# Splitting the first weights behind each layer normalisation one step earlier, into spare activation tiles

## The chip, the core and the metric

The kernel runs on one core of a Trainium2 chip. TensorE (PE) multiplies, VectorE (DVE) and ScalarE (ACT) work on tiles, GpSimd (POOL) can do some of the same work, and SyncE (SP) issues the weight transfers from HBM. Each engine works through its own queue in order. The metric is the device time of one execution in microseconds (us); lower is better.

## What is computed

Two decoder layers on 256 tokens of width 2048, all in float32. Cut to what matters here:

```python
def layer_norm(x, g, b):
    mu = jnp.mean(x, axis=-1, keepdims=True)
    var = jnp.mean(jnp.square(x - mu), axis=-1, keepdims=True)
    return (x - mu) * lax.rsqrt(var + LN_EPS) * g + b

for l in range(2):
    h = gated_deltanet(x, ...) if l == 0 else diff_attention(x, ..., k_sh, v_sh)   # ends in @ w_out or @ w_o
    x = layer_norm(ALPHA * x + h, ln_g[l, 0], ln_b[l, 0])
    x = layer_norm(ALPHA * x + square(relu(x @ w_up[l])) @ w_down[l], ln_g[l, 1], ln_b[l, 1])
    if l == 0:
        k_sh, v_sh = split(x @ w_kv)
return x
```

Four normalisations stand in this order. Behind each of the first three comes a matrix product that needs the whole normalised row: `w_up` of layer 0, `w_kv`, and `w_up` of layer 1. They are called LN1, LN2 and LN3 below. Behind the fourth comes only the output.

## The kernel before, in words

**Tiling.** The 256 tokens are two tiles of 128 (`t` = 0, 1). A product (`gemm`, one entry of `self.plan`) takes 16 weight blocks of 128x1024 (`k` = 0 to 15, one 512 KB transfer each) and makes 1024 output columns, as two groups of 512 (`g` = 0, 1) in PSUM tiles `acc`. Float32 is split in two: `wh` is the weight rounded to float32r by an ACT cast (line 78) and `wl` the rest, by a DVE subtraction (line 79); the activations are split likewise in `xhl` (the normalised stream, features on partitions) or in `blk` tiles (other activations). One block, one `t` and one `g` then take three PE instructions (lines 174 to 176): xh*wh, xh*wl, xl*wh.

**Steps.** `run` walks over steps of 4 to 6 blocks (`cuts`). A step makes the products of its blocks for `t` = 0, then asks `load_weights` for the blocks of the next step, then makes the products for `t` = 1. So while one step multiplies, the next one is transferred and split. `wr` tiles, into which SP transfers, are four; `wh` and `wl` tiles are six each. A transfer can only be issued when the `wr` tile of four blocks before has been split, and a cast only when the `wh` tile of six blocks before has been multiplied. The pool `blk` has 11 tiles of 128x2048.

**The normalisation.** The product ahead of each normalisation ends in `residual`. In its last step of 6 blocks, the products of `t` = 0 come first, those of `t` = 1 after them, one group `g` after the other. As each `acc` is complete, DVE adds it to the residual row `self.r[t]` (line 293) and takes statistics (line 295). When a row tile is complete, `ln_stats` forms the scale in eight small DVE instructions (lines 255 to 256 and 100 to 103), and `ln_apply(ln, t, q)` normalises quarter `q` (512 columns, four blocks `k`): two DVE instructions (lines 265 and 266), then four PE transposes (line 204), an ACT cast and a DVE subtraction into `xhl`. Quarters 0 and 1 of a row tile are applied directly; quarters 2 and 3 of both are applied behind quarters 0 and 1 of `t` = 1.

**Order around it.** `self.after(ins)` puts what is recorded in its block behind `ins` on that engine. `self.hold` is the last instruction of `ln_stats`; the weights split next are put behind it. While `hold` is set, `load_weights` (called with `share`) gives every odd `k` to POOL instead of DVE. The first product behind a normalisation has steps of 6, 5 and 5 blocks. Tile framework and queues keep the recorded order only roughly: a scheduler sets each engine's final order.

Of the kernel before, what the change touches and what calls it, by code (L numbers as in the profile page):

```python
# [11 lines left out]
F32R = mybir.dt.float32r  # L12
# [6 lines left out]
P = 128  # L19
T = 256  # L20
NT = T // P
D = 2048
KD = D // P
DFF = 8192
C = 1024
G = 512
NG = C // G
SC = 4
# [7 lines left out]
class Trunk:  # L36
# [77 lines left out]
    def act_stat(act):  # L114
        return lambda k, part, t: Trunk.act_view(act[k // 4])[:, part, t, k % 4]

    def gemm(self, nk, wsrc, stat, evac, pre=None, rate=1, need=None, cuts=None):

        self.plan.append((nk, wsrc, stat, evac, pre, rate, need, cuts or [SC] * (nk // SC)))

    def run(self):
        steps = [(i, sum(gm[7][:n]), c) for i, gm in enumerate(self.plan) for n, c in enumerate(gm[7])]
        loaded, self.hold = {}, None
        self.load_weights(loaded, *steps[0])
        acc = {}
        for j, (i, s, n) in enumerate(steps):
            nk, _, stat, evac, pre, rate, need, _ = self.plan[i]
            if s == 0:
                acc = {}
                if pre is not None:  # L130
                    pre()
            if need is not None:
                need(s)
            ws = loaded.pop((i, s))
            for t in range(NT):

                turns = [(g,) for g in range(NG)] if s + n >= nk and t == NT - 1 else [range(NG)]
                for gs in turns:
                    for n_, (k, wh, wl) in enumerate(ws):
                        self.product(acc, k, nk, t, gs, wh, wl, stat)  # L140
                        if n_ and self.pending:
                            fn, args = self.pending.popleft()
                            with self.after(self.last):
                                fn(*args)
                    if s + n >= nk:
                        for g in gs:
                            evac(g, t, acc[g, t])
                if t == 0 and j + 1 < len(steps):
                    with self.after(self.hold):
                        self.load_weights(loaded, *steps[j + 1], self.hold is not None)  # L150
                    self.hold = None
                self.pump(rate)

    def load_weights(self, loaded, i, s, n, share=False):
        wsrc = self.plan[i][1]
        ws = []
        for k in range(s, s + n):
            wr = self.raw.tile([P, C], F32, name="wr")
            self.nc.sync.dma_start(wr, wsrc(k))
            wh = self.hi.tile([P, C], F32R, name="wh")  # L160
            wl = self.lo.tile([P, C], F32R, name="wl")
            self.split(wh, wl, wr, self.nc.gpsimd if share and k % 2 else None)
            ws.append((k, wh, wl))
        loaded[i, s] = ws

    def product(self, acc, k, nk, t, gs, wh, wl, stat):
# [120 lines left out]
    def residual(self, n, alpha, ln=None):  # L287


        def ev(gi, t, ps):  # L290
            q = n * NG + gi
            rc = self.r[t][:, q * G : (q + 1) * G]
            self.nc.vector.scalar_tensor_tensor(rc, rc, alpha, ps, op0=ALU.mult, op1=ALU.add)  # L293
            if ln is not None:
                self.nc.vector.bn_stats(ln["st"][t][:, q], rc)
                if q == D // G - 1:
                    self.ln_stats(ln, t)
                    with self.after(ln["end"]):
                        if ln["out"] is not None:
                            self.ln_finish(ln, t, 2 + t)  # L300
                        elif t == 0:
                            self.ln_apply(ln, 0, 0)
                            self.ln_apply(ln, 0, 1)
                        else:
                            self.ln_apply(ln, 1, 0)
                            self.ln_apply(ln, 1, 1)
                            for n_ in range(2, D // G):
                                self.ln_apply(ln, 0, n_)
                                self.ln_apply(ln, 1, n_)
                    self.hold = ln["end"]  # L310

        return ev
# [21 lines left out]
    def mlp(self, w_up, w_down, g, b, out=None):  # L334
        NQ = 4
        FQ = DFF // NQ
        ln = dict(g_src=g, b_src=b, out=out)
        for f in range(NQ):
            h = []

            def up(n, h=h):
                def ev(gi, t, ps):
                    if t == 0:
                        h.append(self.blk(F32R))
                    a = self.sm()
                    self.nc.scalar.activation(a, ps, AF.Relu)  # L346
                    self.nc.vector.tensor_tensor(a, a, a, op=ALU.mult)  # L347
                    self.soon(self.to_features, a, self.act_view(h[n * NG + gi]), t)

                return ev  # L350

            last = f == NQ - 1
            for n in range(FQ // C):
                self.gemm(
                    KD, self.cols(w_up, f * FQ + n * C), self.x_stat, up(n), cuts=[6, 5, 5] if f == n == 0 else None
                )
            for n in range(D // C):
                self.gemm(
                    FQ // P, self.cols(w_down, n * C, f * FQ), self.act_stat(h),
                    self.residual(n, ALPHA if f == 0 else 1.0, ln if last else None),  # L360
                    pre=(lambda: self.ln_load(ln)) if last and n == 0 else None,
                    cuts=self.ends(n) if last else None,
                )
# [395 lines left out]
    def diff_attention(self, w_kv, w_q, lam_params, subln_w, w_o, g, b, out=None):  # L759
# [27 lines left out]
        def heads(name, follow=None):  # L787


            def ev(gi, t, ps):  # L790
                if (gi, t) == (0, 0):
                    st[name] = self.blk().rearrange("p (h t) -> p h t", h=8)
                a = self.sm()
                nc.scalar.copy(a, ps)
                self.soon(turned, gi, t, a)

            def turned(gi, t, a):
                nc.vector.tensor_copy(st[name][:, gi * 4 : gi * 4 + 4, t * P : (t + 1) * P], self.transpose4(a))
                if follow is not None and (gi, t) == (NG - 1, NT - 1):
                    follow()  # L800

            return ev
# [71 lines left out]
        def q_heads(hh):  # L874
            def follow():
                for h in range(0, 8, 2):
                    for tt in range(NT):
                        self.later(score, st["k"], st["q"], hh, h, tt)

            return heads("q", follow)  # L880
# [13 lines left out]
        for hh in range(2):  # L894
            self.gemm(
                KD, self.cols(w_kv, hh * C), self.x_stat, heads("k"), pre=constants if hh == 0 else None,
                cuts=[6, 5, 5] if hh == 0 else None,
            )
            self.gemm(KD, self.cols(w_q, hh * C), self.x_stat, q_heads(hh))
        for hh in range(2):  # L900
# [53 lines left out]
```

## Time and profile before

| | |
|---|---|
| median of 3 runs | 2472.16 us (2465.31 to 2475.14) |
| the profiled execution, its own time | 2465.03 us |
| its span, first to last instruction | 2463.3 us |
| mean granted TensorE clock | 0.992 |
| DVE busy | 1497.2 us (61%) |
| ACT busy | 1078.2 us (44%) |
| POOL busy | 90.3 us (4%) |

The profiled execution lies at the lower end of the runs. A group of instructions in the page stands with its line, its engine, what it writes and reads (out<-in), how often it ran, its busy time and its mean. "idle before, <-releaser" is the time the engine waited and who ended the wait. PE is busy nearly all the time, but a busy PE instruction overlaps the next: a 128x512 product is shown with 0.39 us while the next starts 0.23 us after it.

### The profile page before, as it was taken

Reading aid. Unit: us, or ns where it says so; the run is one execution under the profiler, and the core shown is the slowest. Engines: PE = TensorE matmul, PEld = TensorE weight load, DVE = VectorE, ACT = ScalarE, POOL = GpSimd, SP = SyncE. Lnnn points to the kernel's source line nnn. Section 1 sums busy time; section 2 is a strip of 40 time slices with the busy share of each in tenths; the row PEclk is TensorE's granted clock in tenths of the full one; section 3 lists DMA queues with packets and bytes.
Section 4 is the critical chain, followed back from the end, with each engine's and each line's share of the span. In section 5 each row is a group of like instructions: output and inputs, shape, how many; then the busy total and the mean of one; then the engine's idle time right before and its main releaser. Section 6 shows DMA issues by size and latency. Waiting matters only on the chain.

```text
span 2463.3 us, 30465 instructions
## 1 busy us (share of the span) xinstructions
PE 2416.1 (98%) x11492; PEld 1983.3 (81%) x11492; DVE 1497.2 (61%) x2333; ACT 1078.2 (44%) x1474; POOL 90.3 (4%) x94
## 2 busy tenths in 40 slices
PE   8999999998999999999998999999999999999997
PEld 7888888887888888888887878788788888888886
DVE  4789689667554544545557575665755554555556
ACT  4545345433443433434433464643443443443442
POOL 0010010002000000000002000000200000000001
PEclk9999899999999999999999999999999999999999
DMA  6545345564555556565554545455455555656553
GB/s 229 155 139 175 98 140 160 166 233 158 188 185 191 182 194 222 172 214 182 195 197 146 180 137 171 155 174 167 161 198 195 182 190 186 217 179 214 185 195 121
DMA packets 120211, 438.84 MB, mean 178 GB/s; under 512 B 13760, under 2 KB 13792, under 8 KB 119040
## 3 DMA queue, kind: packets, MB, share of 16 engines
q1 hardware_dynamic: 115920, 420.79, 52.0%
q0 software_dynamic: 2560, 11.13, 1.4%
q10 hardware_dynamic: 1584, 4.98, 0.5%
q8 instruction: 90, 1.47, 0.2%
q14 instruction: 57, 0.47, 0.1%
HBM read 433.70 MB, written 3.15 MB: 177 GB/s over the span
## 4 chain that ended last, share of the span: by engine, by line
PE 90%; DVE 6%; DMA 2%; issue 1%; ACT 1%; POOL 0%; ACTq 0%; POOLq 0%; DVEq 0%
PE acc L174 27%; PE acc L175 27%; PE acc L176 27%; PE ps L204 3%; DVE wl L79 1%; DVE blk L266 1%; DVE blk L265 1%; PE ps L819 1%; ACT wh L78 1%; PE ps L550 1%; DMA wr<-in_gdn_w_in_dram 1%; PE ps L485 1%; DMA wr<-in_mlp_w_up_dram 0%; PE ps L621 0%; PE ps L847 0%
## 5 line engine op out<-in xcount | busy, mean ns | idle before, releaser
L79 DVE TENSOR_TENSOR wl<-wr,wh 128x1024 fp32r<-128x1024 f32 x785 | 954.5, 1227 | 675.0 <-ACT wh L78 632.1
L78 ACT CAST wh<-wr 128x1024 fp32r<-128x1024 f32 x800 | 832.1, 1052 | 945.6 <-PE acc L176 757.2
L174 PE MATMUL acc<-wh,xhl 128*128 128x512 f32 x1920 | 764.3, 398 | 0.0
L175 PE MATMUL acc<-wl,xhl 128*128 128x512 f32 x1920 | 757.7, 395 | 3.2 <-POOL wl L79 3.2
L176 PE MATMUL acc<-wh,xhl 128*128 128x512 f32 x1920 | 754.8, 393 | 0.0
L174 PE MATMUL acc<-wh,blk 128*128 128x512 f32 x1280 | 500.0, 391 | 0.0
L176 PE MATMUL acc<-wh,blk 128*128 128x512 f32 x1280 | 499.4, 390 | 0.0
L175 PE MATMUL acc<-wl,blk 128*128 128x512 f32 x1280 | 499.1, 390 | 0.0
L175 PEld LDWEIGHTS acc<-wl,xhl 128*128 128x128 f32 x1920 | 363.7, 189 | 75.7 <-POOL wl L79 4.4
L174 PEld LDWEIGHTS acc<-wh,xhl 128*128 128x128 f32 x1920 | 363.8, 189 | 73.8 <-issue 1.7
L176 PEld LDWEIGHTS acc<-wh,xhl 128*128 128x128 f32 x1920 | 362.7, 189 | 73.9
L176 PEld LDWEIGHTS acc<-wh,blk 128*128 128x128 f32 x1280 | 240.4, 188 | 50.1
L174 PEld LDWEIGHTS acc<-wh,blk 128*128 128x128 f32 x1280 | 240.4, 188 | 49.5
L175 PEld LDWEIGHTS acc<-wl,blk 128*128 128x128 f32 x1280 | 240.5, 188 | 49.2
L293 DVE SCALAR_TENSOR_TENSOR blk<-blk,acc 128x512 f32<-128x512 f32 x80 | 54.7, 685 | 85.2 <-PE acc L176 85.2
L204 PE MATMUL ps<-ident,sm 128*128 128x128 f32 x512 | 81.3, 275 | 2.5 <-DVE sm L869 1.8
L204 PEld LDWEIGHTS ps<-ident,sm 128*128 128x128 f32 x512 | 61.3, 140 | 27.3 <-PE acc L176 7.1
L78 ACT CAST blk<-ps 128x512 fp32r<-128x512 f32 x80 | 46.8, 585 | 70.9 <-PE ps L204 70.9
L347 DVE TENSOR_TENSOR sm<-sm 128x512 f32<-128x512 f32 x64 | 44.0, 691 | 52.6 <-ACT sm L346 52.2
L79 DVE TENSOR_TENSOR blk<-ps,blk 128x512 fp32r<-128x512 f32 x80 | 55.0, 688 | 30.1 <-ACT blk L78 30.1
L346 ACT ACTIVATE sm<-acc 128x512 f32<-128x512 f32 x64 | 38.2, 597 | 65.4 <-PE acc L176 62.4
L471 DVE SCALAR_TENSOR_TENSOR sm<-blk,g_cw,sm 128x255 f32<-128x255 f32 (+2 forms) x144 | 60.8, 474 | 0.0
(202 smaller groups left out, 1049.7 us busy)
## 6 DMA issues: line engine op xcount, KB each, us to landing
wr<-in_mlp_w_up_dram SPq DMA_DIRECT2D x256, 512.0 KB, 4.7
wr<-in_mlp_w_down_dram SPq DMA_DIRECT2D x256, 512.0 KB, 5.2
wr<-in_gdn_w_in_dram SPq DMA_DIRECT2D x128, 512.0 KB, 4.4
wr<-in_shared_w_kv_dram SPq DMA_DIRECT2D x64, 512.0 KB, 5.1
wr<-in_gdn_w_out_dram SPq DMA_DIRECT2D x32, 512.0 KB, 5.4
wr<-in_diff_w_q_dram SPq DMA_DIRECT2D x32, 512.0 KB, 4.6
wr<-in_diff_w_o_dram SPq DMA_DIRECT2D x32, 512.0 KB, 4.7
blk<-in_ln_g_dram POOLq DMA_DIRECT2D x4, 1024.0 KB, 7.2
```

What stands on the lines that cost most here:

```text
L78: self.nc.scalar.copy(hi, src)
L79: (engine or self.nc.vector).tensor_tensor(lo, src, hi.bitcast(F32), op=ALU.subtract)
L174: mm(ps, xh, wh[:, c], start=(k == 0), stop=False)
L175: mm(ps, xh, wl[:, c], start=False, stop=False)
L176: self.last = mm(ps, xl, wh[:, c], start=False, stop=(k == nk - 1))
L204: self.nc.tensor.transpose(pt[:, i], src[:, i * P : (i + 1) * P], self.ident)
L265: v.scalar_tensor_tensor(xc, xc, ln["mv", t][:, 0:1], ln["g"][:, c], op0=ALU.subtract, op1=ALU.mult)
L266: v.scalar_tensor_tensor(xc, xc, ln["rs", t], ln["b"][:, c], op0=ALU.mult, op1=ALU.add)
L293: self.nc.vector.scalar_tensor_tensor(rc, rc, alpha, ps, op0=ALU.mult, op1=ALU.add)
L346: self.nc.scalar.activation(a, ps, AF.Relu)
L347: self.nc.vector.tensor_tensor(a, a, a, op=ALU.mult)
L471: v_.scalar_tensor_tensor(y[:, i, d:], u[:, : T - d], w(j), y[:, i, d:], op0=ALU.mult, op1=ALU.add)
```

## The change

1. Products behind LN1, LN2 and LN3 are marked `ahead` and take steps of 5, 6 and 5 blocks.
2. Before the last step of the product ahead of the normalisation starts, `load_weights(..., big=True)` transfers and splits the five blocks of the first step behind it. They go into `blk` tiles, `wh` in one half and `wl` in the other, so no `wh`/`wl` tile is needed. At that point five `blk` tiles are free: three of the 11 not in use, and two of the four activation tiles, whose blocks have been multiplied.
3. No weight is split on POOL any more.
4. Quarters 2 and 3 of the normalisation are kept in `self.rest` as (0,2), (1,2), (0,3), (1,3) in (t, q), and are recorded inside the load of the second step: one behind its third block, one behind its sixth, the other two at the end.

```diff
-    def gemm(self, nk, wsrc, stat, evac, pre=None, rate=1, need=None, cuts=None):
+    def gemm(self, nk, wsrc, stat, evac, pre=None, rate=1, need=None, cuts=None, ahead=False):
-        self.plan.append((nk, wsrc, stat, evac, pre, rate, need, cuts or [SC] * (nk // SC)))
+        cuts = [5, 6, 5] if ahead else cuts or [SC] * (nk // SC)
+        self.plan.append((nk, wsrc, stat, evac, pre, rate, need, cuts, ahead))
...
             ws = loaded.pop((i, s))
+            if j + 1 < len(steps) and steps[j + 1][1] == 0 and self.plan[steps[j + 1][0]][8]:
+                self.load_weights(loaded, *steps[j + 1], big=True)
             for t in range(NT):
...
-                if t == 0 and j + 1 < len(steps):
+                if t == 0 and j + 1 < len(steps) and steps[j + 1][:2] not in loaded:
                     with self.after(self.hold):
-                        self.load_weights(loaded, *steps[j + 1], self.hold is not None)
+                        self.load_weights(loaded, *steps[j + 1])
...
-    def load_weights(self, loaded, i, s, n, share=False):
+    def load_weights(self, loaded, i, s, n, big=False):
...
-            wh = self.hi.tile([P, C], F32R, name="wh")
-            wl = self.lo.tile([P, C], F32R, name="wl")
-            self.split(wh, wl, wr, self.nc.gpsimd if share and k % 2 else None)
+            if big:
+                both = self.blk(F32R)
+                wh, wl = both[:, :C], both[:, C:]
+            else:
+                wh = self.hi.tile([P, C], F32R, name="wh")
+                wl = self.lo.tile([P, C], F32R, name="wl")
+            self.split(wh, wl, wr)
             ws.append((k, wh, wl))
+            if self.rest and not big and (k - s) % 3 == 2:
+                fn, args = self.rest.pop(0)
+                fn(*args)
+        while self.rest and not big:
+            fn, args = self.rest.pop(0)
+            fn(*args)
         loaded[i, s] = ws
...
-                            for n_ in range(2, D // G):
-                                self.ln_apply(ln, 0, n_)
-                                self.ln_apply(ln, 1, n_)
+                            self.rest = [(self.ln_apply, (ln, t_, n_)) for n_ in range(2, D // G) for t_ in range(NT)]
```

**What moves on the engines.** Outside the three normalisations, each engine's instructions keep their order; the three places change alike, and LN1 is shown. Lines 265, 266, 293, 295 and 204 of before are 282, 283, 310, 312 and 221 of the change; lines 174 to 176 are 191 to 193.

DVE before, where the last step ahead of LN1 is split (`wl`) and the statistics of `t` = 0 begin (`blk<-blk,acc` is the residual, `ln_st` the statistics):

```order
L79 TENSOR_TENSOR wl<-wr,wh 128x1024 x10
L293 SCALAR_TENSOR_TENSOR blk<-blk,acc 128x512 x2
L295 BN_STATS ln_st<-blk 128x6 x2
L255 BN_AGGR ln_mv<-ln_st 128x2
L256 TENSOR_SCALAR ln_rs<-ln_mv 128x1
```

DVE of the change at the same place (`blk<-wr,blk` is the `wl` half of a block split early; the third `blk<-blk,acc` belongs to `t` = 1):

```order
L79 TENSOR_TENSOR wl<-wr,wh 128x1024 x10
L79 TENSOR_TENSOR blk<-wr,blk 128x1024 x3
L310 SCALAR_TENSOR_TENSOR blk<-blk,acc 128x512
L79 TENSOR_TENSOR blk<-wr,blk 128x1024 x2
L312 BN_STATS ln_st<-blk 128x6
L310 SCALAR_TENSOR_TENSOR blk<-blk,acc 128x512
L312 BN_STATS ln_st<-blk 128x6
L310 SCALAR_TENSOR_TENSOR blk<-blk,acc 128x512
L272 BN_AGGR ln_mv<-ln_st 128x2
L312 BN_STATS ln_st<-blk 128x6
L273 TENSOR_SCALAR ln_rs<-ln_mv 128x1
```

Five subtractions now stand ahead of the statistics of `t` = 0, two of them between its first residual and its first statistics, and a residual with its statistics of `t` = 1 stand ahead of the scale of `t` = 0.

PE before, at the end of the last step ahead of LN1 (`acc<-wh,blk` multiplies activations of that product, `acc<-wh,xhl` is the first product behind the normalisation, `ps<-ident,blk` the eight transposes of quarters 0 and 1 of `t` = 0):

```order
L175 MATMUL acc<-wl,blk 128x512
L204 MATMUL ps<-ident,blk 128x128 x8
L176 MATMUL acc<-wh,blk 128x512
L174 MATMUL acc<-wh,blk 128x512
L175 MATMUL acc<-wl,blk 128x512
L176 MATMUL acc<-wh,blk 128x512
L174 MATMUL acc<-wh,blk 128x512
L175 MATMUL acc<-wl,blk 128x512
L176 MATMUL acc<-wh,blk 128x512
L174 MATMUL acc<-wh,blk 128x512
L175 MATMUL acc<-wl,blk 128x512
L176 MATMUL acc<-wh,blk 128x512
```

PE of the change there (`acc<-blk,xhl` multiplies a block split early):

```order
L193 MATMUL acc<-wh,blk 128x512
L191 MATMUL acc<-wh,blk 128x512
L192 MATMUL acc<-wl,blk 128x512
L193 MATMUL acc<-wh,blk 128x512
L221 MATMUL ps<-ident,blk 128x128 x8
L191 MATMUL acc<-blk,xhl 128x512
L192 MATMUL acc<-blk,xhl 128x512
L191 MATMUL acc<-blk,xhl 128x512
L192 MATMUL acc<-blk,xhl 128x512
L193 MATMUL acc<-blk,xhl 128x512 x2
L191 MATMUL acc<-blk,xhl 128x512
```

The transposes now stand behind the last product of the step, with nothing between them and the first product that needs them.

DVE before, from the last normalisation of quarters 2 and 3 (`blk<-blk,ln_mv` and `blk<-blk,ln_rr`, lines 265 and 266) to the second step's weights:

```order
L265 SCALAR_TENSOR_TENSOR blk<-blk,ln_mv 128x512 x2
L266 SCALAR_TENSOR_TENSOR blk<-blk,ln_rr 128x512
L79 TENSOR_TENSOR xhl<-ps,xhl 128x512
L266 SCALAR_TENSOR_TENSOR blk<-blk,ln_rr 128x512
L265 SCALAR_TENSOR_TENSOR blk<-blk,ln_mv 128x512
L79 TENSOR_TENSOR xhl<-ps,xhl 128x512
L266 SCALAR_TENSOR_TENSOR blk<-blk,ln_rr 128x512
L79 TENSOR_TENSOR xhl<-ps,xhl 128x512
L79 TENSOR_TENSOR wl<-wr,wh 128x1024
L79 TENSOR_TENSOR xhl<-ps,xhl 128x512
L79 TENSOR_TENSOR wl<-wr,wh 128x1024 x8
```

DVE of the change there, from the first block of the second step on:

```order
L79 TENSOR_TENSOR wl<-wr,wh 128x1024
L79 TENSOR_TENSOR xhl<-ps,xhl 128x512 x2
L79 TENSOR_TENSOR wl<-wr,wh 128x1024 x2
L282 SCALAR_TENSOR_TENSOR blk<-blk,ln_mv 128x512
L79 TENSOR_TENSOR wl<-wr,wh 128x1024
L283 SCALAR_TENSOR_TENSOR blk<-blk,ln_rr 128x512
L79 TENSOR_TENSOR wl<-wr,wh 128x1024 x2
L79 TENSOR_TENSOR xhl<-ps,xhl 128x512
L282 SCALAR_TENSOR_TENSOR blk<-blk,ln_mv 128x512 x2
L283 SCALAR_TENSOR_TENSOR blk<-blk,ln_rr 128x512 x2
L282 SCALAR_TENSOR_TENSOR blk<-blk,ln_mv 128x512
L283 SCALAR_TENSOR_TENSOR blk<-blk,ln_rr 128x512
```

All six blocks of the second step now stand ahead of three of the four late quarters, on the engine that does both.

More of the change, by code (lines that the diff above doesn't have):

```diff
@@ L115, in act_stat @@
         return lambda k, part, t: Trunk.act_view(act[k // 4])[:, part, t, k % 4]
-    def gemm(self, nk, wsrc, stat, evac, pre=None, rate=1, need=None, cuts=None):
-        self.plan.append((nk, wsrc, stat, evac, pre, rate, need, cuts or [SC] * (nk // SC)))
+    def gemm(self, nk, wsrc, stat, evac, pre=None, rate=1, need=None, cuts=None, ahead=False):
+        cuts = [5, 6, 5] if ahead else cuts or [SC] * (nk // SC)
+        self.plan.append((nk, wsrc, stat, evac, pre, rate, need, cuts, ahead))
     def run(self):
         steps = [(i, sum(gm[7][:n]), c) for i, gm in enumerate(self.plan) for n, c in enumerate(gm[7])]
-        loaded, self.hold = {}, None
+        loaded, self.hold, self.rest = {}, None, []
         self.load_weights(loaded, *steps[0])
@@ L126, in run @@
         for j, (i, s, n) in enumerate(steps):
-            nk, _, stat, evac, pre, rate, need, _ = self.plan[i]
+            nk, _, stat, evac, pre, rate, need = self.plan[i][:7]
             if s == 0:
@@ L353, in mlp @@
             for n in range(FQ // C):
-                self.gemm(
-                    KD, self.cols(w_up, f * FQ + n * C), self.x_stat, up(n), cuts=[6, 5, 5] if f == n == 0 else None
-                )
+                self.gemm(KD, self.cols(w_up, f * FQ + n * C), self.x_stat, up(n), ahead=f == n == 0)
             for n in range(D // C):
@@ L896, in diff_attention @@
                 KD, self.cols(w_kv, hh * C), self.x_stat, heads("k"), pre=constants if hh == 0 else None,
-                cuts=[6, 5, 5] if hh == 0 else None,
+                ahead=hh == 0,
             )
```

## The prediction

> **What bounds the kernel now.** I read the page's first lines, then PE's waits, then the timelines of the engines around LN1, and compared LN2 and LN3 with it.
>
> From the page, and from PE's waits over the whole span (who waited, us in total, times, longest):
>
> ```profile
> PE 2416.1 (98%) x11492; PEld 1983.3 (81%) x11492; DVE 1497.2 (61%) x2333; ACT 1078.2 (44%) x1474; POOL 90.3 (4%) x94
> ...
> PE ps L204 <- DVE blk L266: 14.2, 6, 3.5
> ...
> PE acc L175 <- POOL wl L79: 3.2, 3, 1.7
> ...
> PE ps L204 <- issue: 1.7, 1, 1.7
> ```
>
> PE is the bound. The three waits belong to the normalisations alone and sum to 14.2 + 3.2 + 1.7 = **19.1 us**; no change of this place can win much more. PE's timeline at LN1 shows them (start, length, idle before in brackets):
>
> ```profile
> 576.64 0.39 PE L175 MATMUL acc<-wl,blk 128*128 128x512 f32 x1
> 577.17 1.27 PE L204 MATMUL ps<-ident,blk 128*128 128x128 f32 x8
> 578.20 0.48 PE L176 MATMUL acc<-wh,blk 128*128 128x512 f32 x1
> ...
> 580.36 0.39 PE L176 MATMUL acc<-wh,blk 128*128 128x512 f32 x1
> 580.59 0.39 PE L174 MATMUL acc<-wh,xhl 128*128 128x512 f32 x1
> ...
> 588.51 0.50 PE L175 MATMUL acc<-wl,xhl 128*128 128x512 f32 x1 [0.74 <-POOL wl L79]
> ...
> 591.65 0.52 PE L204 MATMUL ps<-ident,blk 128*128 128x128 f32 x3 [1.71 <-issue]
> ...
> 604.31 0.63 PE L204 MATMUL ps<-ident,blk 128*128 128x128 f32 x4 [3.54 <-DVE blk L266]
> ```
>
> PE enters LN1's product at 580.59 without a stop: the eight transposes fit between products. It stops three times later: for a block split on POOL (0.74), for `t` = 1's scale (1.71), for the last late quarters (3.54). DVE's and POOL's timelines say why:
>
> ```profile
> 564.79 1.23 DVE L79 TENSOR_TENSOR wl<-wr,wh 128x1024 fp32r<-128x1024 f32 x1 [0.82 <-ACT wh L78]
> 570.50 1.37 DVE L293 SCALAR_TENSOR_TENSOR blk<-blk,acc 128x512 f32<-128x512 f32 x2 [4.48 <-PE acc L176]
> 571.78 1.28 DVE L295 BATCH_NORM_STATS2 ln_st<-blk 128x6 f32<-128x512 f32 x2
> 573.10 0.27 DVE L255 BATCH_NORM_AGGREGATE ln_mv<-ln_st 128x2 f32<-128x24 f32 x1
> 573.39 0.15 DVE L256 TENSOR_SCALAR ln_rs<-ln_mv 128x1 f32<-128x1 f32 x1
> ...
> 575.00 1.41 DVE L265 SCALAR_TENSOR_TENSOR blk<-blk,ln_mv 128x512 f32<-128x512 f32 x2
> 576.32 1.41 DVE L266 SCALAR_TENSOR_TENSOR blk<-blk,ln_rr 128x512 f32<-128x512 f32 x2
> ...
> 598.16 2.90 DVE L265 SCALAR_TENSOR_TENSOR blk<-blk,ln_mv 128x512 f32<-128x512 f32 x1
> ...
> 601.59 2.58 DVE L266 SCALAR_TENSOR_TENSOR blk<-blk,ln_rr 128x512 f32<-128x512 f32 x1
> ...
> 606.42 2.35 DVE L79 TENSOR_TENSOR wl<-wr,wh 128x1024 fp32r<-128x1024 f32 x2
> ```
>
> ```profile
> 597.63 2.89 POOL L79 TENSOR_TENSOR wl<-wr,wh 128x1024 fp32r<-128x1024 f32 x1 [9.17 <-ACT wh L78]
> 601.28 2.34 POOL L79 TENSOR_TENSOR wl<-wr,wh 128x1024 fp32r<-128x1024 f32 x1 [0.77 <-ACT wh L78]
> ```
>
> DVE idles 4.48 us ahead of the statistics and is then full. Its instructions of 0.75 us take 2.90 and 2.58 while POOL splits: that is the 3.54 us stop.
>
> **What goes.** The POOL wait (3.2 in all) goes, with its splits. DVE gets five splits more per normalisation, 1.13 each back to back (606.42: 2.35 - 1.22), 5.7 us, but loses about 2.15 + 1.83 us of such stretching, and the five come ahead of the statistics, where 4.48 us were free. The stops of 1.71 and 3.54 shrink accordingly. A subtraction into half a `blk` tile is not in the trace; it has the shape and types of the row at 606.42, and I take that. It could not well be less; were it stretched as at 598.16 it would be 2.9, but no POOL split runs beside it any more. Transfers and casts keep their number and order on SP and ACT; the four `wr` tiles stay.
>
> **What comes: the first place.** ACT and the transfers, with the landing times of the four transfers issued ahead of LN1, LN2 and LN3 in turn:
>
> ```profile
> 563.71 1.05 ACT L78 CAST wh<-wr 128x1024 fp32r<-128x1024 f32 x1 [0.99 <-DMA wr<-in_gdn_w_out_dram]
> 575.94 2.00 ACT L78 CAST wh<-wr 128x1024 fp32r<-128x1024 f32 x2 [11.18 <-PE acc L176]
> ```
>
> ```profile
> L159 SPq DMA_DIRECT2D wr<-in_mlp_w_up_dram x4: 327/328/328, 561.3 to 566.0; - x4
> ...
> DMA to landing us min/median/max: 3.7/4.7/5.0
> ```
>
> ```profile
> L159 SPq DMA_DIRECT2D wr<-in_shared_w_kv_dram x4: 328/328/328, 1284.9 to 1289.6; - x4
> ...
> DMA to landing us min/median/max: 3.8/5.1/5.6
> ```
>
> ```profile
> L159 SPq DMA_DIRECT2D wr<-in_mlp_w_up_dram x4: 327/328/328, 1706.4 to 1711.0; - x4
> ...
> DMA to landing us min/median/max: 4.3/4.9/5.2
> ```
>
> Before, these blocks landed by 570.5 and lay until a `wh` tile came free (the 11.18 us). Now they are cast on landing. LN1: the first lands at 561.3 + 3.7 = 565.0, its cast (1.05, 0.1 behind the landing) ends at 566.1, its split at 567.4. Only then is a `wr` tile free for the **fifth** block: landing 4.7 later at 572.1, cast to 573.3. Splits 2 and 3 run to 571.2, the first residual to 571.9, split 4 to 573.0, split 5 from 573.3 to 574.4. Behind it, in the order shown with the change, stand three statistics (0.66 each), two residuals (0.64), the aggregate (0.29), the scale (575.00 - 573.39 = 1.61), two L265 (1.32) and one L266 (0.75): 7.2 us. The first transpose can go at 574.4 + 7.2 + 0.1 = **581.7**. PE, without the transposes inside the step (578.20 - 576.64 - 0.23 = 1.33, and 0.09 behind them), ends it at 580.59 - 1.42 = 579.2. So PE now stops **2.5 us** where it did not stop. LN2 and LN3 start from these rows:
>
> ```profile
> 1294.12 1.37 DVE L293 SCALAR_TENSOR_TENSOR blk<-blk,acc 128x512 f32<-128x512 f32 x2 [4.56 <-PE acc L176]
> ```
>
> ```profile
> 1715.64 1.37 DVE L293 SCALAR_TENSOR_TENSOR blk<-blk,acc 128x512 f32<-128x512 f32 x2 [4.65 <-PE acc L176]
> ```
>
> The same steps: LN2's first lands at 1288.7, its split ends at 1291.1, the fifth lands 5.1 later, split 5 ends at 1298.5, the transpose goes at 1305.8; PE ends its step 8.7 us after the residual row, at 1302.8: 3.0. LN3: 1710.7, 1713.1, + 4.9, 1720.3, 1727.6 against 1724.3: 3.3. Together **8.8 us** of new stop.
>
> **The second place.** Let B be the first product behind the normalisation. DVE: two `xhl` (0.6 each), statistics and scale of `t` = 1 (2.6), two L265, first L266: done at B + 5.9, where PE is after 26 products (26 x 0.227): 0.1 of stop in place of 1.71. Then one split and the two `xhl` of `t` = 1, splits 2 and 3, a quarter with split 4 in it, splits 5 and 6. Block 6 of this step needs the `wr` tile of split 2, free at B + 10.0; 4.7 to land, 1.2 to cast: split 6 ends at B + 17.0, and the L266 of quarter (1,2) ends 2.7 later (0.6 + 2 x 0.66 + 0.75) at B + 19.7. PE wants it after the rest of `t` = 0 and 1 and 16 products, at B + 18.7: 1.1 of stop, and 0.2 for the quarter behind it. So 1.4 per normalisation, **4.2 us** in all.
>
> Weights behind that: the next step's four transfers are then long issued, and its casts wait for `wh` tiles as before: nothing. ACT's five early casts (5.3 us) fit into its 11.18 idle: nothing. The `blk` tiles are free in the program's order; were they not, ACT would wait (a rival).
>
> **The clock.** The granted clock in stretches behind a stop (column PEclk, the last but two):
>
> ```profile
> 1310.00:1316.00 6.00, 2.86 (x12) 1.72 (x10) 5.69 (x13) 0.58 (x1) 2.36 (x1) 0.99 0.74 240
> 1316.00:1319.00 3.00, 2.69 (x10) 2.40 (x11) 2.28 (x5) 1.17 (x2) 0.00 (x0) 0.50 0.10 38
> 1329.80:1332.80 3.00, 2.84 (x9) 2.48 (x10) 2.84 (x5) 1.03 (x2) 0.00 (x0) 0.50 0.15 18
> ...
> 605.00:608.40 3.40, 3.40 (x16) 2.82 (x15) 3.40 (x4) 1.62 (x2) 0.00 (x0) 1.00 0.42 107
> 1749.60:1752.60 3.00, 3.00 (x10) 2.52 (x11) 2.84 (x4) 1.29 (x2) 0.00 (x0) 0.50 0.20 31
> ```
>
> After stops it fell to half for 3 us, twice in LN2, once in LN3, never in LN1. 3 us at half do 1.5 of work; part of it PE waited anyway, so I take 1.0 each: 3.0 before. The change's stops are fewer but one is long; I take half, 1.5 (bounds 0 and three times 1.5, 4.5).
>
> The Trainium skill ("TensorE: Matmul & The Clock Gate", Part 1: The HAM clock gate) says the clock halves after a whole idle window of about 3.4 us, free-running. By it none of the stops above would lower the clock and the sum would be 1.5 lower. This trace does not bear it out: the fall at 1316 came after 6 us with 2.86 of PE work in them.
>
> **The sum.** Before 19.1 + 3.0 = 22.1; after 8.8 + 4.2 + 1.5 = 14.5: 7.6 us won. The profiled execution took 2465.03, so 2457.4 in its place. It lies 7.1 below the median of 2472.16; the runs shown spread over 10, so I subtract from the median: **2464 us**.
>
> **Rivals.**
> - *Short transfers.* All landings over the span, in one row:
>
> ```profile
> DMA to landing us min/median/max: 3.1/4.8/13.4
> ```
>
> With 3.1 for fifth and sixth blocks, split 5 waits for DVE alone (LN1 0.3, LN2 0.3, LN3 0.9 less) and split 6 too (1.3 less in each): 5.4 more won, and 1.5 if the clock holds: 14.5, so 2458. For: fewer transfers are under way at the second place. Against: three others are at the first.
> - *The clock holds* at every stop: no half-clock stretch is left, all else as summed: 9.1 won, 2463. For: LN1's row at 605 with 1.00 behind a stop of 3.54. Against: the three rows with 0.50. It is also what the Trainium skill's rule, named above, would give.
> - *Late blocks, slower than before.* DVE works in order, so each us that the fifth and sixth blocks land later than 4.7 to 5.1 holds up the normalisation behind them, once at each place: 6 us per us of landing. The 7.6 are gone at about 1.3 later, near 6.2 us; at 8.3 the kernel is at 2484, slower by 0.5%. Against: the medians above; for: the 13.4, and that the order leaves no slack.
> - *Not early at all.* A `blk` tile comes free only at the step's end, ACT's casts wait there, and the five splits fall behind the normalisation: about 2472. Against: the last step needs only two of the four activation tiles.
>
> **Chances.** Forecast 0.42, short transfers 0.25, clock holds 0.15, late 0.14, not early 0.04. A measurement of this kernel tells about 0.5% (12.4 us) from no change. Short transfers exceed it mostly (0.24), the forecast at its edge (0.06): faster 0.30. Late blocks are slower by as much in half their cases: 0.07. The rest, 0.63, is within it. The range takes in the two best cases and the late blocks up to 6.2 us, with a few us for the spread of runs: 2452 to 2474.
>
> **What would show it.** Right: DVE's subtractions ahead of the first residual; no POOL in these stretches, L265 and L266 at 0.75; PE waiting for L266 (line 283) at the first transposes, some 2.5 to 3.3 us, and about 1 at quarters (1,2) and (0,3); the casts into `blk` released by transfers. Wrong: no stop at the first transposes, or one far over 4 us; ACT's early casts released by PE; a fifth transfer issued later than the end of the first early split; new stops outside the three places.

## The result, and the profile after

| | before | change |
|---|---|---|
| median of 17 runs each, us | 2467.98 (2459.38 to 2477.98) | 2447.07 (2444.38 to 2464.07) |
| ratio, 95% interval | | 0.9929 [0.9913, 0.9945] |
| the profiled execution's own time, us | 2465.03 | 2446.75 |
| its span, us | 2463.3 | 2445.0 |
| mean granted TensorE clock | 0.992 | 0.995 |

The change makes the kernel faster, by 0.71% (0.55% to 0.87%), about 17.5 us. Forecast were 7.6 us, and a time of 2464 us with 2452 to 2474 as its range; the measured 2447.07 lies below it.

PE's waits of the change from the first normalisation to behind the third (who waited, us in total, times, longest; a row of the attention stage is left out):

```profile
PE ps L221 <- DVE blk L283: 7.0, 2, 4.0
PE ps L221 <- issue: 2.3, 1, 2.3
...
```

The wait for POOL is gone, and three stops are left where there were ten: one at each normalisation, 7.0 + 2.3 = 9.3 us in all. PE's timeline shows where the one of LN1 stands (start, length, idle before in brackets):

```profile
572.57 0.39 PE L193 MATMUL acc<-wh,blk 128*128 128x512 f32 x1
575.27 1.27 PE L221 MATMUL ps<-ident,blk 128*128 128x128 f32 x8 [2.31 <-issue]
576.57 0.50 PE L191 MATMUL acc<-blk,xhl 128*128 128x512 f32 x1
...
595.80 1.33 PE L221 MATMUL ps<-ident,blk 128*128 128x128 f32 x8
```

It is the first of the two places that the prediction named: the first transposes, behind the last product of the step before. At the second, the late quarters (595.80 and later), there is next to nothing: the product ahead of that row began at 595.29 and was shown with 0.39, so PE sat idle for 0.12. The other two normalisations have the same row:

```profile
1295.59 1.94 PE L221 MATMUL ps<-ident,blk 128*128 128x128 f32 x8 [3.01 <-DVE blk L283]
...
1712.19 1.11 PE L221 MATMUL ps<-ident,blk 128*128 128x128 f32 x4 [3.99 <-DVE blk L283]
```

DVE's timeline at LN1 says what the transposes wait for:

```profile
560.03 1.22 DVE L79 TENSOR_TENSOR blk<-wr,blk 128x1024 fp32r<-128x1024 f32 x1 [0.66 <-ACT blk L78]
562.41 2.49 DVE L79 TENSOR_TENSOR blk<-wr,blk 128x1024 fp32r<-128x1024 f32 x2 [1.16 <-ACT blk L78]
564.82 0.68 DVE L310 SCALAR_TENSOR_TENSOR blk<-blk,acc 128x512 f32<-128x512 f32 x1
565.42 1.22 DVE L79 TENSOR_TENSOR blk<-wr,blk 128x1024 fp32r<-128x1024 f32 x1
567.13 1.23 DVE L79 TENSOR_TENSOR blk<-wr,blk 128x1024 fp32r<-128x1024 f32 x1 [0.49 <-ACT blk L78]
568.27 0.69 DVE L312 BATCH_NORM_STATS2 ln_st<-blk 128x6 f32<-128x512 f32 x1
...
574.42 1.40 DVE L283 SCALAR_TENSOR_TENSOR blk<-blk,ln_rr 128x512 f32<-128x512 f32 x2
...
591.89 1.23 DVE L79 TENSOR_TENSOR wl<-wr,wh 128x1024 fp32r<-128x1024 f32 x1 [0.54 <-ACT wh L78]
...
594.96 1.41 DVE L283 SCALAR_TENSOR_TENSOR blk<-blk,ln_rr 128x512 f32<-128x512 f32 x2
```

The fourth and fifth early subtractions (565.42, 567.13) stand ahead of the first statistics, the fifth waiting for its cast, and from there DVE works without a pause to the first quarter, at 575.2. Lines 282 and 283 are not stretched in the three places (two of them 1.40 or 1.41, none alone over 0.75): nothing runs on POOL beside them.

**Where the 18.3 us between the two profiled spans went.** Not all of them are the change's. The last gate of the DeltaNet stage, on ACT, before and in the change:

```profile
491.42 0.60 ACT L737 ACTIVATE sm<-acc 128x512 f32<-128x512 f32 x1
```

```profile
485.08 0.60 ACT L750 ACTIVATE sm<-acc 128x512 f32<-128x512 f32 x1
```

6.3 us lie ahead of this point, where the two programs are the same, and 12.0 behind it. A stretch of 20 us inside that stage, of before, of before run once more (below) and of the change, tells the reason (PE's busy time and count first; the granted clock PEclk is the last column but two):

```profile
268.00:288.00 20.00, 20.00 (x126) 15.92 (x125) 5.63 (x6) 5.09 (x7) 0.00 (x0) 0.50 0.31 91
```

```profile
268.00:288.00 20.00, 20.00 (x245) 17.27 (x241) 9.06 (x18) 8.01 (x23) 0.00 (x0) 1.00 0.45 148
```

```profile
268.00:288.00 20.00, 20.00 (x197) 16.80 (x194) 9.23 (x28) 8.82 (x25) 0.00 (x0) 1.00 0.38 120
```

The execution of before on which the prediction was built had TensorE at half speed there. The clock records have such a spell, 20.5 us long, in five of the twelve executions profiled for this study, with kernels of every kind among them. The last gate then comes at 491.4 to 497.0, otherwise at 484.0 to 486.9. The runs show it too: most kernels' times fall into two or three groups some 10 us apart, and the medians differ by 20.9, more than the ratio says, since ten of the change's seventeen lie in its lowest group while before's median stands between groups. So two readings that this spell does not touch are used from here on: the time from the last gate to the span's end, called the **rest**, and the lowest run of each kernel.

### The profile page after: what moved, and what is told of

Its sections match the earlier page's. It is cut to its first block, busy times and chain, and to the rows that moved or that the text cites. A ratio compares the mean times of both kernels' runs of the same rounds, so it can differ in the third digit from the quotient of the medians.

```text
span 2445.0 us, 30450 instructions
## 1 busy us (share of the span) xinstructions
PE 2406.5 (98%) x11492; PEld 1976.3 (81%) x11492; DVE 1494.4 (61%) x2348; ACT 1080.3 (44%) x1474; POOL 48.3 (2%) x79
## 3 DMA queue, kind: packets, MB, share of 16 engines
HBM read 433.70 MB, written 3.15 MB: 179 GB/s over the span
## 4 chain that ended last, share of the span: by engine, by line
PE 90%; DVE 5%; DMA 2%; issue 1%; ACT 1%; SPq 0%; ACTq 0%; DVEq 0%; POOLq 0%
PE acc L191 27%; PE acc L192 27%; PE acc L193 27%; PE ps L221 3%; DVE wl L79 1%; PE ps L832 1%; DMA wr<-in_gdn_w_in_dram 1%; PE ps L563 1%; ACT wh L78 1%; DMA wr<-in_shared_w_kv_dram 1%; PE ps L498 1%; PE ps L860 0%; PE ps L871 0%; DVE blk L282 0%; DVE blk L600 0%
## 5 line engine op out<-in xcount | busy, mean ns | idle before, releaser
L78 ACT CAST wh<-wr 128x1024 fp32r<-128x1024 f32 x785 | 817.1, 1053 | 914.6 <-PE acc L193 748.3
L191 PE MATMUL acc<-wh,xhl 128*128 128x512 f32 x1860 | 737.0, 396 | 0.0
L192 PE MATMUL acc<-wl,xhl 128*128 128x512 f32 x1860 | 731.0, 393 | 0.1
L193 PE MATMUL acc<-wh,xhl 128*128 128x512 f32 x1860 | 729.0, 392 | 0.0
L191 PEld LDWEIGHTS acc<-wh,xhl 128*128 128x128 f32 x1860 | 351.0, 189 | 70.9 <-issue 1.7
L193 PEld LDWEIGHTS acc<-wh,xhl 128*128 128x128 f32 x1860 | 350.1, 188 | 71.7
L192 PEld LDWEIGHTS acc<-wl,xhl 128*128 128x128 f32 x1860 | 350.9, 189 | 69.4 <-issue 1.0
```

The lines of the kernel that those rows point to most:

```text
L78: self.nc.scalar.copy(hi, src)
L191: mm(ps, xh, wh[:, c], start=(k == 0), stop=False)
L192: mm(ps, xh, wl[:, c], start=False, stop=False)
L193: self.last = mm(ps, xl, wh[:, c], start=False, stop=(k == nk - 1))
```

## The experiments

All were run beside the kernel before, on the same chip. For each profiled execution, "stops" is the sum of PE's idle times of 0.1 us or more at the three normalisations, and "half" the time at half clock there:

| execution | ratio, 95% interval | lowest run | rest | stops | half | rest - stops - 0.4 x half |
|---|---|---|---|---|---|---|
| before | | 2459.38 | 1971.9 | 19.3 | 10.2 | 1948.5 |
| before again | 1.001 [0.9987, 1.0033] | 2459.58 | 1978.0 | 19.0 | 27.2 | 1948.1 |
| change | 0.9929 [0.9913, 0.9945] | 2444.38 | 1959.9 | 9.6 | 10.2 | 1946.2 |
| change, second time | 0.9937 [0.9913, 0.9962] | 2445.17 | 1960.7 | 9.1 | 13.6 | 1946.2 |
| change, third time | 0.991 [0.9874, 0.9945] | 2444.12 | 1958.6 | 9.0 | 6.8 | 1946.9 |
| before, no POOL | 0.9951 [0.993, 0.9971] | 2451.22 | 1965.4 | 12.2 | 17.0 | 1946.4 |
| change, late quarters at once | 0.9939 [0.9916, 0.9963] | 2445.38 | 1957.4 | 8.6 | 6.8 | 1946.1 |
| change, nothing early | 0.9969 [0.9949, 0.9988] | 2448.43 | 1963.6 | 11.0 | 13.6 | 1947.2 |
| two blocks behind | 0.9904 [0.9881, 0.9926] | 2436.86 | 1949.5 | 3.3 | 0 | 1946.2 |
| two behind, second time | 0.9906 [0.9873, 0.9939] | 2437.70 | 1949.6 | 3.4 | 0 | 1946.2 |
| one block behind | 0.9924 [0.9895, 0.9954] | 2439.28 | 1952.5 | 4.8 | 0 | 1947.7 |
| two behind, late quarters at once | 0.9921 [0.9893, 0.9949] | 2441.17 | 1954.1 | 5.5 | 0 | 1948.6 |

Over all twelve the rest is within 1.3 us of 1947.3 + stops + 0.4 x half. The 0.4 is fitted to these rows; a us at half clock can cost at most 0.5, and less where PE would have waited anyway. The stage ahead of the last gate, where all the programs are the same, gives a price that no stop of the normalisations enters: the twelve executions have 3.4 to 30.7 us at half clock there, and their gates come at 483.2 + 0.44 x that time, each within 0.9 us.

**Before, run once more.** No edit; it shows what two executions of one kernel differ by.

> The kernel before, against itself. Theory A (the part of the 17 to 21 us that the three normalisations do not show, about 6 us ahead of LN1 in the pair of profiles, is a lower clock in the DeltaNet stage that comes and goes from execution to execution): ratio 1.000 within 0.3%; executions from 2459 to 2478, longer ones at a lower granted clock; the time from the span's start to LN1's first residual is not fixed at 570.5 and may be 564. Theory B (the change makes the DeltaNet stage itself faster): ratio 1.000 too, but LN1's first residual stays at 570 whatever the time of the execution.

The time is the same, and LN1's first residual starts at 564.92 instead of 570.50, as the first of the two theories asked. But the rest is 6.1 us longer. The three normalisations with the clock, first as first profiled, then here:

```profile
560.00:620.00 60.00, 53.79 (x249) 43.17 (x248) 46.99 (x64) 23.63 (x27) 14.08 (x5) 1.00 0.47 155
1270.00:1350.00 80.00, 72.78 (x322) 59.23 (x321) 55.90 (x71) 30.38 (x34) 13.69 (x5) 0.96 0.49 157
1690.00:1760.00 70.00, 63.76 (x285) 51.41 (x285) 51.04 (x67) 26.28 (x30) 14.04 (x5) 0.98 0.51 166
```

```profile
560.00:620.00 60.00, 53.35 (x228) 42.69 (x227) 43.90 (x62) 20.83 (x24) 13.77 (x5) 0.91 0.42 136
1270.00:1350.00 80.00, 73.50 (x318) 59.27 (x317) 55.01 (x71) 29.61 (x33) 13.71 (x5) 0.94 0.48 158
1690.00:1760.00 70.00, 64.00 (x281) 51.78 (x280) 51.23 (x67) 26.09 (x29) 13.75 (x5) 0.95 0.49 160
```

The stops are alike to 0.3 us, and the clock is lower in all three places, LN1 among them, which the prediction counted as spared. One profile is a sample of the clock, not its rule.

**Before without POOL splits.** The first of the change's parts alone:

```diff
-                        self.load_weights(loaded, *steps[j + 1], self.hold is not None)
+                        self.load_weights(loaded, *steps[j + 1])
```

> Before, with no split on POOL (all on DVE), nothing early. Theory A (half of what was won is the end of the POOL splits, which stretched VectorE's 0.75 us instructions to 2.6 to 2.9): the 3.5 us stops at the late quarters fall to under 1 us, the 0.7 to 1.7 us waits for POOL go, the 1.7 us stops at t = 1 grow to about 2.5; 8 to 11 us won, ratio about 0.996. Theory B (what counts is that splits leave VectorE's queue early; without that the five go on DVE and eat the gain): the stops only move, ratio 0.999 to 1.003.

PE's waits:

```profile
PE ps L204 <- DVE blk L266: 7.6, 3, 3.9
PE ps L204 <- issue: 3.5, 1, 3.5
...
PE acc L175 <- DVE wl L79: 0.9, 2, 0.7
```

This part by itself wins 12.1 us (0.49% of 2469.31, with 7.2 to 17.3 as the interval). That is over half of what the change wins: 9.5 of 15.2 by the rest, 8.2 of 15.0 by the lowest runs. The stretched L265 and L266 are back at 0.74, and the stops of 3.54 at the late quarters are gone. DVE now makes all of the splits, four of them ahead of `t` = 1's scale, and the stop there grows from about 1.7 to between 3.5 and 3.9 in each normalisation. The sum goes from 19.3 to 12.2. POOL's help cost more than it gave. The Trainium skill ("SBUF — State Buffer", SBUF: two separate sides) says that a DVE instruction with two SBUF inputs and a GpSimd one that reads SBUF hold a shared port pair in turn, for the whole instruction. The prediction's rows agree: a DVE instruction that takes 0.75 here took 2.90, beside one of 2.89 on POOL.

**The change with the late quarters applied at once**, directly behind quarters 0 and 1 of `t` = 1, as before:

```diff
-                            self.rest = [(self.ln_apply, (ln, t_, n_)) for n_ in range(2, D // G) for t_ in range(NT)]
+                            for n_ in range(2, D // G):
+                                self.ln_apply(ln, 0, n_)
+                                self.ln_apply(ln, 1, n_)
```

> The change, with quarters 2 and 3 applied directly as before instead of between the weights of the second step. Theory A (the early splits and the end of POOL do it; the place of the late quarters hardly matters): the first stops of 2.3 to 4.0 us stay, the late quarters show no stop, no wait for the second step's weights: time within 0.15% of the change, ratio to before about 0.993. Theory B (the interleaving is needed): the second step's weights come late, PE waits for wl or wh by 1 to 4 us at each normalisation, ratio to before 0.995 to 0.998.

It can't be told from the change, by the time or the stops (8.6, all at the first place). Putting quarters between weights wins nothing here.

**The change with nothing early**: no POOL, late quarters between weights, steps of 5, 6 and 5, but the first weights split behind the scale as before.

```diff
-            if j + 1 < len(steps) and steps[j + 1][1] == 0 and self.plan[steps[j + 1][0]][8]:
+            if False:
```

> The change without the early splits: steps of 5, 6 and 5, no POOL, late quarters between the weights of the second step; the first step's weights are split behind the scale as before. Theory A (nothing early means the five splits stand between the two scales, as with POOL taken away alone): stops of 3 to 4 us at the transposes of t = 1, the late quarters without a stop, half-clock windows in all three places; ratio to before 0.995 to 0.997, like the run without POOL splits. Theory C (the interleaving is worth something by itself): 0.993 or less.

The stops are 3.44, 4.13 and 3.15, each at `t` = 1's scale: with 0.3 of small ones 11.0, near the 12.2 without POOL alone. So the early split, on top of the other two parts, saves 11.0 - 9.2 (mean of the change's three executions) = 1.8 us of stops, and 3.9 us by the rest. It does not remove the stop. It moves it from `t` = 1's scale to `t` = 0's transposes.

**Two blocks behind the scale.** If splits 4 and 5 ahead of the statistics make the stop at the transposes, three blocks early and two behind `t` = 0's scale should take most of it:

```diff
-                self.load_weights(loaded, *steps[j + 1], big=True)
+                i_, s_, n_ = steps[j + 1]
+                self.load_weights(loaded, i_, s_, 3, big=True)
...
-                if t == 0 and j + 1 < len(steps) and steps[j + 1][:2] not in loaded:
+                if t == 0 and j + 1 < len(steps) and steps[j + 1][:2] in loaded:
+                    i_, s_, n_ = steps[j + 1]
+                    head = loaded[i_, s_]
+                    with self.after(self.hold):
+                        self.load_weights(loaded, i_, s_ + 3, n_ - 3, big=True)
+                    self.hold = None
+                    loaded[i_, s_] = head + loaded.pop((i_, s_ + 3))
+                elif t == 0 and j + 1 < len(steps):
```

> The change, with only the first three blocks split ahead of the statistics of t = 0 and the other two behind its scale. Theory A (the new stop at the first transposes comes from splits 4 and 5 standing ahead of the statistics in VectorE's order): that stop, 9.3 us in the three, goes to under 0.5 us each; the two splits now delay the scale of t = 1, so a stop of about 2 us shows at its transposes; in all 1 to 4 us less than the change, ratio to before about 0.992. Theory B (VectorE's work between the two scales is the bound whatever its order): the same total of stops as the change, about 10 us, ratio 0.993.

DVE's timeline at LN1, and PE's waits:

```profile
563.89 2.44 DVE L79 TENSOR_TENSOR blk<-wr,blk 128x1024 fp32r<-128x1024 f32 x2 [1.38 <-ACT blk L78]
566.24 1.28 DVE L318 SCALAR_TENSOR_TENSOR blk<-blk,acc 128x512 f32<-128x512 f32 x2
567.44 1.28 DVE L320 BATCH_NORM_STATS2 ln_st<-blk 128x6 f32<-128x512 f32 x2
...
571.98 1.41 DVE L291 SCALAR_TENSOR_TENSOR blk<-blk,ln_rr 128x512 f32<-128x512 f32 x2
573.30 1.22 DVE L79 TENSOR_TENSOR blk<-wr,blk 128x1024 fp32r<-128x1024 f32 x1
```

```profile
PE ps L229 <- DVE blk L291: 2.0, 3, 1.4
...
PE ps L229 <- issue: 1.3, 1, 1.3
```

The statistics follow the third split, and the stops fall to 3.3 us, by more than the 1 to 4 us that were expected. The expected stop at `t` = 1's transposes did not come. But 1.30, 1.36 and 0.31 us are left at the first transposes, where under 0.5 each was expected. PE's timeline at LN1 shows why:

```profile
571.14 0.39 PE L200 MATMUL acc<-wl,blk 128*128 128x512 f32 x1
572.83 1.27 PE L229 MATMUL ps<-ident,blk 128*128 128x128 f32 x8 [1.30 <-issue]
573.86 0.48 PE L201 MATMUL acc<-wh,blk 128*128 128x512 f32 x1
...
576.02 0.39 PE L201 MATMUL acc<-wh,blk 128*128 128x512 f32 x1
576.24 0.39 PE L199 MATMUL acc<-blk,xhl 128*128 128x512 f32 x1
```

The scheduler has put the eight transposes ten products ahead of the step's end again, as before, where the change has them behind the last product. PE stops for them while ten products, 2.3 us at 0.23 each, stand ready behind them. All of this version's stops at the first transposes, 1.6 us at most, would fit into these ten; no run placed the transposes behind them. No half clock is left in the three places:

```profile
560.00:620.00 60.00, 58.70 (x276) 47.61 (x275) 46.42 (x71) 24.68 (x29) 0.00 (x0) 1.00 0.52 171
1270.00:1350.00 80.00, 78.32 (x367) 63.84 (x366) 58.63 (x81) 34.89 (x39) 0.00 (x0) 1.00 0.52 171
1690.00:1760.00 70.00, 69.59 (x328) 56.70 (x327) 55.96 (x81) 31.90 (x38) 0.00 (x0) 1.00 0.52 173
```

By the rest, 10 us shorter than the change's, and by the lowest run, 2436.86 against 2444.12, this version beats both kernels. It was run once more, and **the change twice more**, the third time beside it. The expectations count the time from the first of the last four gates, 5.7 us ahead of the one used here:

> The version with two blocks split behind the scale, beside the change. Theory A (stops, and the clock's falls that follow them, are all that differs): from the last DeltaNet gate to the end 1955 +- 2 us, stops of 3 to 4 us in the three places and no half-clock window in them; 8 to 12 us faster than the change at the same granted clock in the DeltaNet stage. Against it: a half-clock window in a place without a stop of over 1.5 us, or the same time with stops gone.

> The change once more, to see which of its profile's lines stand and which are that execution's own. Theory A (stops at the first transposes are fixed by queues, the clock's falls are not): first stops of 2.2 to 4.1 us in the same order LN1 < LN2 < LN3, no stop over 0.5 us at the late quarters; half-clock time inside the three places anywhere from 0 to 14 us, and executions of equal granted clock 12 to 15 us under those of before.

> The change, on the same chip and in the same rounds as the version with two blocks behind the scale. From the last DeltaNet gate to the end of the span: 1966 +- 3 us (two executions so far gave 1965.7 and 1966.4), made of about 1953 + the stops in the three places (9 to 10 us) + 0.4 of the half-clock time there.

The rest repeats to 0.1 us here and to 2.1 in the change; on the expectations' count it is 1955.3 here and 1964.3 in the change's third execution, both as expected. The medians of that last pair (2447.13 and 2445.39) would say the opposite: five of the six runs of two behind took 2446.8 to 2450.0, and its profile has the spell of 20.5 us in DeltaNet at 270. The sixth took 2437.70. Of the change's six, four took 2444.1 to 2445.5.

**One block behind** (3 becomes 4 in the edit above):

> The change, with four blocks split ahead of the statistics of t = 0 and only the fifth behind its scale. Theory A (each split ahead of the statistics costs the first transposes what exceeds the slack): first stop about 0.5 to 1.3 us, the stop at t = 1 about 1 us, no half-clock window: total near the version with two behind, 2437 to 2441. Theory B' (the fifth block's late landing alone makes the first stop): first stop under 0.3 us as with two behind, 2435 or less.

Stops of 0.8 to 1.2 each, 4.8 in all, between the two: 3.1 at the first transposes, as expected, and 1.8 at the late quarters of LN1 and LN2 instead of `t` = 1's transposes. Here the first transposes stand behind the step's last product, as in the change. Measured against the end of the step's products, they come 2.4 to 4.1 us late in the change's three executions, 1.0 to 1.4 late with one block behind, and 0.8 to 1.8 ahead of it with two (there ten products are still to come). So both the fourth and the fifth split take their part.

**Two behind, with the late quarters at once**:

> Two blocks split behind the scale, as in e4, and the late quarters applied directly as in e2. Theory A (the interleaving hardly matters): same as e4 within 0.1%, 2437 to 2441. Theory B (without the stop at the first transposes PE reaches the second step's weights sooner, so the interleaving now matters): waits for wl of 1 us or more at the start of the second step, 2441 to 2446.

PE now stops 0.3 to 0.95 for weights of the second step, 2.5 in all and 5.5 with the stops at the first transposes, and the rest is 4.5 us longer than with two behind alone, two of which are stops. The lowest run, 2441.17, lies where the two theories meet; the second asked for waits of 1 us or more, and the longest is 0.95. The intervals of the two overlap widely.

## Why the prediction was wrong

By terms, from the rows above (before: mean of two executions; change: mean of three):

| | predicted | measured |
|---|---|---|
| stops before | 19.1 | 19.2 |
| first place, after | 8.8 | 9.3, 9.1, 8.6 |
| second place, after | 4.2 | 0.3, 0, 0.3 |
| clock, before | 3.0 | 0.4 x 18.7 = 7.5 |
| clock, after | 1.5 | 0.4 x 10.2 = 4.1 |
| won | 7.6 | 10.0 + 3.4 = 13.4; by the rest 15.2 |

- **What goes: right.** The POOL wait and the stretching are gone, and the 1.71 and the 3.54 with them. No new POOL or `blk` wait came, and the early casts are released by transfers.
- **The first place: right in mechanism and sum.** At LN1 the chain was forecast to take 581.7 - 565.1 = 16.6 us from the first early cast to the first transpose. It took 575.27 - 558.95 = 16.3; a stop of 2.5 was forecast, and 2.31 came. Which normalisation has the longest stop changes from one execution to the next (3.55, 2.57, 2.99 in the second, where LN1 was expected to stay the shortest), the sum hardly does. That splits 4 and 5 make it is shown by moving them, first one and then both. The first and the fifth early cast wait for their transfers, as forecast:

```profile
558.95 1.05 ACT L78 CAST blk<-wr 128x1024 fp32r<-128x1024 f32 x1 [0.83 <-DMA wr<-in_mlp_w_up_dram]
...
566.04 1.06 ACT L78 CAST blk<-wr 128x1024 fp32r<-128x1024 f32 x1 [1.05 <-DMA wr<-in_mlp_w_up_dram]
```

- **The second place: the term was mis-sized**, 4.2 for 0.2 on average. (Its own parts, 1.1 and 0.2 at each normalisation, add up to 3.9.) With B the start of the first product behind the normalisation (576.57 at LN1), quarter (1,2) was forecast done at B + 19.7 and wanted by PE at B + 18.7. In the row of LN1 it is done at 594.96 + 0.74 = 595.70, which is B + 19.1, and PE came at 595.68. A landing was taken as 4.7 where the block of this place took 4.05 (issued 586.69, landed 590.74), so its split ended 0.5 sooner, at 593.12; DVE still idled 0.54 for it. With 1.0 between the two forecasts, errors of a few tenths in three rows made the whole term. The rival of short transfers had the size of this place right, but by luck: it took 3.1 for a landing, where 4.05, 4.10 and 3.67 came. It had the first place wrong.
- **The clock: one execution was taken as the rule.** Half clock was counted as 9 us before; two executions have 10.2 and 27.2. It was priced at a third of a us for each; the fit says 0.4. Nor did the clock hold, as a rival had it: the change has 6.8 to 13.6 us at half. The 19.1 named as about the most that this place could give left the clock out: two blocks behind win 25.4 by the rest, 22.5 by the lowest runs.
- **The base.** The gain was taken from a median of three runs that stood 4.2 us above the median of seventeen. This shifts the predicted time, 2464, not the gain.

The stops, 3.9 us better than forecast and nearly all of it at the second place, and the clock, 1.9 better, take the 7.6 to 13.4. The 1.8 from there to 15.2 is unexplained, and of the size of the fit's spread. The ratio's 17.5 us (13.6 to 21.5) holds the 15.2; the 13.4 is just below it. The lowest runs differ by 2459.38 - 2444.38 = 15.0. The medians differ by 5.7 more than the 15.2; with the 4.2 of the base they make up 9.9 of the 17.5 us between 2472.16 - 7.6 = 2464.6 and 2447.07. No run shows how much of these 5.7 is the change's.

Open are what sets off the spell in DeltaNet, and what the version with two blocks behind would take with its transposes placed behind the last product of the step.

## What to carry to other kernels

Work moved ahead of a chain is free only as far as the engine idles there: three splits fitted into DVE's gap ahead of the statistics, and the fourth and fifth became the new stop. Helping a busy engine with one that slows it can be worth less than nothing, so try the removal alone first. Before a gain of some 0.5% is read off two profiles, align them at a landmark outside the change, and take a second execution of the kernel before.

## What the runs showed of the hardware

- Stretches at half clock last 3.4, 6.8 or 20.5 us in the clock records, multiples of about 3.4. The one of 20.5 comes in a stage where PE has no stop that the records show (20.00 of 20.00 busy above). Up to the last gate, 491.42 - 485.90 = 5.5 us separate the two executions of before (20.5 us at half clock ahead of it against 6.8), and 495.56 - 483.99 = 11.6 two of the change (27.3 against 3.4). By the 0.44 us of all twelve, a spell of 20.5 costs some 9 us, an estimate.
- The Trainium skill ("TensorE: Matmul & The Clock Gate", Part 1: The HAM clock gate) asks for a whole idle window of about 3.4 us ahead of a fall. Here shorter stops sufficed. In the four executions with one long stop at each normalisation (the change's three, and late quarters at once), the eight stops of 2.57 to 4.05 us all had a fall at them or within 2 us behind, four of them being shorter than 3.4 (2.57 to 3.01), and the four of 2.21 to 2.32 had none. This row shows the 3.4 us at a stop of 2.79 in the change's third execution:

```profile
574.10:577.50 3.40, 2.87 (x11) 2.49 (x12) 2.65 (x5) 1.17 (x2) 0.00 (x0) 0.50 0.00 0
```

- It is no fixed threshold: before's stop of 3.54 at LN1 had no fall in one execution and one of 3.4 us in the other, and its second execution had a fall at a stop of 1.71 that came 1.4 us behind one of 1.24. Where the longest stop was 1.6 us (the four executions with one or two blocks behind) there was none.
